# Attention layer on one core: later residues and roots, earlier row sums, and input rows added onto a second copy of the first product

## Chip, core and metric

The kernel runs on one core of one Trainium2 chip, as one launch. The metric is the device time of one execution in microseconds (us). In the profile PE is the matrix engine (TensorE), PEld its weight loads, DVE is VectorE, ACT ScalarE, POOL GpSimd and SP the queue that issues most transfers.

## The reference

One layer on 2048 tokens (a grid 64 wide) of width 1024, all in float32: a norm, one projection into q, k, v and gate, attention of each token over 8 rows by 16 columns of neighbours with a bias, a gate, an output projection, the residual sum and a last norm.

```python
g, w_in, rpb, w_out = layers[0]
h = rmsnorm(x, g)                          # y * rsqrt(mean(y*y) + 1e-6) * g
o, gate = neighbourhood_mixer(h, w_in, rpb)  # 16 heads of 64; softmax over 8 x 16 neighbours
x = x + (o * jax.nn.silu(gate)) @ w_out
return rmsnorm(x, norm_f)
```

## The kernel before

**Products.** Each float32 operand is split into a high part (rounded to the matrix engine's format) and a residue, and each product of two operands is made of three matmuls (high by high, high by residue, residue by high). Large products are made block by block as seven products of sums of blocks in place of eight (the products P stand in the order 1, 6, 2, 7, 5, 4, 3). A *form* `f` is a sum of blocks or a raw block, split for the matrix engine: ACT rounds it (`f<-raw`), DVE takes the residue (`f<-raw,f`). After a product DVE adds its bank to an earlier one (`u<-pp,acc`), or finishes an output.

**Order.** The kernel writes its whole order out: every engine runs its instructions in the order in which the program records them, with semaphores between engines. There is no scheduler. What a program line is recorded after is therefore what it stands behind on its engine.

**Stage one** (`stage_one`, to about 400 us) makes q, k, gate and values. `step(i)` records product i of a sequence, and `forms(i + lead)` makes the forms that many products ahead. `diagonal(c)` builds a diagonal matrix of row scales for `spread_rstd`: DVE writes `dg`, ACT rounds it to `dgh`, and DVE takes the residue `dgl`. **Stage two** (`stage_two`) goes on with the rest of the projections.

**Attention** runs in 32 cycles, one for each pair of heads and each eighth of the grid. A cycle records normalisation of the last scores, a filler of other matmuls on PE (`feed`, among them the output projection of the first row tiles, `po`), transposes `ph` of the probabilities (`turns`: PE transposes, three banks copied to `pta` by DVE and three by ACT), new scores `s`, and values `o`. The output projection of a row tile ends with `y<-po,xr` on DVE (bank plus input rows), a square with row sum on ACT, and then `finish(n)`: a *root* (eight short DVE rows of one column, lines 1457 to 1464, a reciprocal square root without ACT), a *scale* (two DVE rows of 512 columns, line 1472) and a *send*. `run_roots` and `run_scales` record what is due, once in a cycle: the scales first, of the roots that the last cycle made, then new roots. `rooted` holds the tiles that have a root and no scale yet.

**Output projection in pairs** (`rows_by_seven`, from about 905 us). Row tiles 6 to 15 are taken in PAIRS of two, each pair m as one block matrix of two rows by two columns, with the seven products `rows_product(m, P)`. The first three pairs are interleaved, and the last two follow. `on(i, f, ...)` records f behind step i of the sequence. `load_rows_of` loads a block of gated outputs, `sum_rows` makes S1 to S4, `form_rows` the forms, `add_rows` a finished output (`y<-py,...`, line 1430). `load_rest_of` loads input rows for the residual sum, `add_rest` adds them by an accumulating transfer on POOL onto a tile that holds a partial sum. `land_T2` and `land_T4` load sums of blocks of the weights. For these tiles the root takes three short DVE rows and a square root on ACT. `store(key, lag, f)` records f when a counter of finished work has moved on by `lag`.

Of the kernel before, what the change touches and what calls it, by code (L numbers as in the profile page):

```python
# [11 lines left out]
F32 = mybir.dt.float32  # L12
# [65 lines left out]
def build(ctx, tc, x, xr, xt, wg, bias, w_out, n0, nf, out):  # L78
# [141 lines left out]
    def diagonal(c, home=ev, late=False):  # L220
        dg = home([128, 512], F32, "dg")
        for i in range(4):
            to, f = dg[:, i * 128:(i + 1) * 128], rt[:, 4 * c + i:4 * c + i + 1]
            if late:
                nc.scalar.activation(to, ident, AF.Copy, scale=f)
            else:
                nc.vector.tensor_scalar(to, ident, f, None, op0=OP.mult)
        dgs[c] = h, l = home([128, 512], F32R, "dgh"), home([128, 512], F32R, "dgl")
        nc.scalar.activation(h, dg, AF.Copy)
        nc.vector.tensor_tensor(l, dg, h.bitcast(F32), OP.subtract)  # L230

    def spread_rstd(c):
        p = bank(512, "prb")
# [376 lines left out]
    def stage_one():  # L610
# [830 lines left out]
    def finish(n):  # L1441
# [129 lines left out]


    PAIRS = [(n, n + 1) for n in range(PLAIN, tiles - 2, 2)] + [(tiles - 1, tiles - 2)]
    A, F, B, U, R, T4 = {}, {}, {}, {}, {}, {}
    TF = {}
    plain_of = {"B11": (0, 0), "B21": (1, 0), "B22": (1, 1)}

# [42 lines left out]
    def load_rest_of(m, j, k):  # L1620
        n = PAIRS[m][j]
        RES[n, k] = (qp if (j, k) == (1, 0) else rbp)([128, 512], F32, "xr")
        nc.sync.dma_start(RES[n, k], x[n * 128:n * 128 + 128, 512 * k:512 * k + 512])

    def add_rest(n, j, to):
        nc.gpsimd.dma_start(to, x[n * 128:n * 128 + 128, 512 * j:512 * j + 512], accum_op=OP.add)

    def rows_product(m, P):
        n0, n1 = PAIRS[m]
        if P in (1, 6, 5):  # L1630
            B[m, P] = bank(512, "py")
            for Q in {1: (2,), 6: (7, 4), 5: (3,)}[P]:
                B[m, Q] = B[m, P]
        t = F.pop((m, P))
        f = uses[P][1]
        for k in range(4):
            c = slice(k * 128, k * 128 + 128)
            xh, xl = TF[f][k]
            for i, (a, b) in enumerate(((0, xh), (0, xl), (1, xh))):
                nc.tensor.matmul(B[m, P], t[:, a, c], b, start=P in (1, 6, 5) and k == 0 and i == 0, stop=k == 3 and i == 2,  # L1640
                                 skip_group_check=True)
                due(1)
        if P == 1:
            U[m, 1] = (xp if m == 2 else ep)([128, 512], F32, "p1")
            nc.scalar.activation(U[m, 1], B[m, 1], AF.Copy)
        elif P == 2:
            add_rows(n0, 0, B[m, 2])
        elif P in (6, 7):
            U[m, P] = xp([128, 512], F32, "u")
            nc.vector.tensor_tensor(U[m, P], B[m, P], U[m, 1], OP.add)  # L1650
            to = (n0, 1) if P == 6 else (n1, 1)
            if P == 6:
                RES[to] = U[m, 6]
                add_rest(n0, 1, U[m, 6])
            else:
                xr_ = RES.pop(to)
                nc.vector.tensor_tensor(U[m, 7], U[m, 7], xr_, OP.add)
                RES[to] = U[m, 7]
                add_rest(n1, 0, U[m, 1])
                RES[n1, 0] = U[m, 1]  # L1660
        elif P == 5:
            add_rows(n1, 1, B[m, 5])
        elif P == 4:
            add_rows(n1, 0, B[m, 4])
            finish(n1)
        else:
            add_rows(n0, 1, B[m, 3])
            finish(n0)

    def rows_by_seven():  # L1670
        for f, (r, c) in plain_of.items():
            TF[f] = [(woh[4 * r + k, c], wol[4 * r + k, c]) for k in range(4)]
        E, LEAD = 3, 5
# [7 lines left out]
        def on(i, f, *a):  # L1681
            todo.setdefault(i, []).append((f, a))
# [9 lines left out]
        for m in range(E, len(PAIRS)):  # L1692
            s = seq.index((m, 6)) - 1
            for d, f in ((-12, "A11"), (-10, "A21"), (-9, "A22"), (-7, "A12")) if m == E else \
                    ((-9, "A21"), (-8, "A22"), (-7, "A11"), (-6, "A12")):
                on(s + d, load_rows_of, m, f)
            for d, f in ((-5, "S1"), (-4, "S2"), (-3, "S3"), (-1, "S4")):
                on(s + d, sum_rows, m, f)
            on(s - 2, load_rest_of, m, 0, 0)
            on(s, load_rest_of, m, 1, 1)  # L1700
        for i, m in ((5, 0), (7, 1), (11, 2)):
            on(i, load_rest_of, m, 1, 1)
        for i, s in enumerate(seq):
            if i >= 2 * E:
                on(i - LEAD, form_rows, *s)
        for f in ("A21", "A22"):
            load_rows_of(1, f, vh)
        for m in range(E):
            load_rest_of(m, 0, 0)
        land_T4()  # L1710
        for m in range(E):
            form_rows(m, 2)
# [68 lines left out]
    for m in range(cycles + 1):  # L1781
# [3 lines left out]
        if m:  # L1785
            due_here = []
            quiet[0] = True
            if a < 12 and m > 8 and m % 2:
                normalise(2 * m - 1, True, lambda: due_here.append(split_rows() or consume(1, turn=True)))
            else:  # L1790
                normalise(2 * m - 1, True)
            run_scales()
            if a > 12:
                run_roots()
            elif not rows_due():
                run_roots(1)
# [12 lines left out]
        else:  # L1809
            feed(a * 0.6)  # L1810
# [61 lines left out]
```

## Time and profile before

| | |
|---|---|
| runs | 1009.82, 1009.84, 1011.5 us |
| median | 1009.84 us |
| profiled execution | 1009.61 us |
| its span | 1007.8 us, 1.8 us less than the execution |
| granted clock of PE | 0.999 |
| PE busy | 996.5 us, 6904 matmuls |
| DVE busy | 773.9 us |
| ACT busy | 519.4 us |
| POOL busy | 145.9 us |

A row of the timeline has start, duration, engine, line, operation, output and inputs, size and count; in brackets stands how long the engine was idle before it and what ended that. A row with a count over 1 groups neighbours that are alike.

### The profile page before, as it was taken

Reading aid. Unit: us, or ns where it says so; the run is one execution under the profiler, and the core shown is the slowest. Engines: PE = TensorE matmul, PEld = TensorE weight load, DVE = VectorE, ACT = ScalarE, POOL = GpSimd, SP = SyncE. Lnnn points to the kernel's source line nnn. Section 1 sums busy time; section 2 is a strip of 40 time slices with the busy share of each in tenths; the row PEclk is TensorE's granted clock in tenths of the full one; section 3 lists DMA queues with packets and bytes.
Section 4 is the critical chain, followed back from the end, with each engine's and each line's share of the span. In section 5 each row is a group of like instructions: output and inputs, shape, how many; then the busy total and the mean of one; then the engine's idle time right before and its main releaser. Section 6 shows DMA issues by size and latency. Waiting matters only on the chain. (4 is left out here: it accounts for less than half of the span.)

```text
span 1007.8 us, 19563 instructions
## 1 busy us (share of the span) xinstructions
PE 996.5 (99%) x6904; PEld 797.1 (79%) x6904; DVE 773.9 (77%) x1708; ACT 519.4 (52%) x1267; POOL 145.9 (14%) x228
## 2 busy tenths in 40 slices
PE   9999999999999999999999999999999999999997
PEld 6887888888888888888888777777777777778876
DVE  5899888987666866676765776778788888787876
ACT  7872244455534423343433465667767657563443
POOL 0000001321100000000000133233333323221100
PEclk9999999999999999999999999999999999999999
DMA  8945347777957755655566787879987679799453
GB/s 294 343 124 165 128 140 254 236 255 255 355 152 226 246 155 169 209 187 183 203 198 203 212 275 231 266 236 284 285 247 261 203 232 302 221 362 356 136 158 105
DMA packets 150122, 228.19 MB, mean 226 GB/s; under 512 B 13640, under 2 KB 65096, under 8 KB 150024
## 3 DMA queue, kind: packets, MB, share of 16 engines
q1 hardware_dynamic: 148152, 223.92, 69.1%
q0 software_dynamic: 1440, 2.62, 1.7%
q8 instruction: 54, 0.88, 0.3%
q10 hardware_dynamic: 432, 0.40, 0.1%
q14 instruction: 44, 0.36, 0.1%
HBM read 160.83 MB, written 66.06 MB: 225 GB/s over the span
## 5 line engine op out<-in xcount | busy, mean ns | idle before, releaser
L441 PE MATMUL pp<-h,f 128*128 128x512 f32 x576 | 185.3, 389 | 0.0
L1307 POOL TENSOR_SCALAR x<-x,st 128x360 f32<-128x360 f32 (+5 forms) x192 | 106.3, 570 | 530.0 <-DVE st L1300 529.7
L441 PE MATMUL pp<-t,f 128*128 128x512 f32 x702 | 171.9, 389 | 1.1 <-DVE u L454 1.1
L441 PEld LDWEIGHTS pp<-t,f 128*128 128x128 f32 x702 | 131.6, 188 | 29.2 <-ACT f L423 1.5
L1295 ACT ACTIVATE x<-x,st 128x360 f32<-128x360 f32 (+5 forms) x256 | 134.2, 526 | 26.4 <-DVE st L1289 26.4
L441 PEld LDWEIGHTS pp<-h,f 128*128 128x128 f32 x576 | 108.1, 188 | 22.4
L441 PE MATMUL pp<-l,f 128*128 128x512 f32 x288 | 112.1, 389 | 0.0
L1289 DVE CUSTOM_DVE_ANT_0 x<-s,em 128x360 f32<-128x360 f32 (+5 forms) x256 | 102.5, 454 | 2.1 <-PE s L1280 1.4
L424 DVE TENSOR_TENSOR f<-raw,f 128x512 fp32r<-128x512 f32 x105 | 75.6, 725 | 20.3 <-ACT f L423 20.2
L1354 PEld LDWEIGHTS o<-pta,vt 120*64 120x64 f32 (+2 forms) x1024 | 68.7, 137 | 22.7 <-DVE st L1289 15.2
L1354 PE MATMUL o<-pta,vt 120*64 120x192 f32 (+5 forms) x1024 | 83.4, 316 | 0.3 <-issue 0.3
L423 ACT ACTIVATE f<-raw 128x512 fp32r<-128x512 f32 x105 | 63.3, 622 | 38.3 <-DVE raw L430 22.3
L1324 DVE COPY pta<-ph 120x512 f32<-120x512 f32 (+5 forms) x96 | 56.0, 637 | 32.8 <-PE ph L1335 32.6
L1280 PE MATMUL s<-kt,q 64*64 64x360 f32 (+5 forms) x1024 | 78.8, 420 | 1.2 <-DVE y L1430 1.0
L1326 ACT ACTIVATE pta<-ph 120x512 f32<-120x512 f32 (+5 forms) x96 | 46.8, 558 | 62.5 <-PE ph L1335 62.4
L441 PEld LDWEIGHTS pp<-l,f 128*128 128x128 f32 x288 | 54.1, 188 | 11.3
L1280 PEld LDWEIGHTS s<-kt,q 64*64 64x64 f32 x1024 | 41.6, 131 | 23.1 <-ACT pta L1326 6.1
L605 PE MATMUL pv<-wh,t 128*128 128x512 f32 x176 | 56.2, 389 | 0.0
L441 PE MATMUL pp<-sixths,f 128*128 128x512 f32 x198 | 52.7, 389 | 0.0
L462 POOL TENSOR_TENSOR tmp<-tmp,rb 128x512 f32<-128x512 f32 x18 | 29.3, 1629 | 161.8 <-DVE tmp L459 132.7
L1640 PE MATMUL py<-woh,f 128*128 128x512 f32 x160 | 50.9, 390 | 0.9 <-DVE y L1430 0.9
L1335 PEld LDWEIGHTS ph<-ident,x 64*120 64x120 f32 (+2 forms) x1408 | 42.5, 128 | 11.3 <-issue 9.5
(222 smaller groups left out, 1864.2 us busy)
## 6 DMA issues: line engine op xcount, KB each, us to landing
raw<-in_wg_dram SPq DMA_DIRECT2D x124, 256.0 KB, 5.0
row<-in_xr_dram SPq DMA_DIRECT2D x34, 256.0 KB, 5.5
vd<-v SPq DMA_DIRECT2D x32, 256.0 KB, 3.4
sgd<-sg SPq DMA_DIRECT2D x32, 256.0 KB, 5.5
q<-qd SPq DMA_DIRECT2D x32, 256.0 KB, 5.6
sgt<-sgd SPq DMA_DIRECT2D x32, 256.0 KB, 6.6
ogd<-og SPq DMA_DIRECT2D x32, 256.0 KB, 3.3
kt<-kd SPq DMA_DIRECT2D x16, 480.0 KB, 6.6
```

Of the source, the lines that this page charges most:

```text
L423: nc.scalar.activation(t[:, 0], src, AF.Copy)
L424: nc.vector.tensor_tensor(t[:, 1], src, t[:, 0].bitcast(F32), OP.subtract)
L441: nc.tensor.matmul(B[n, P], t[:, int(m == 2), c], x[k][int(m == 1)], start=P in (1, 6, 5) and k == 0 and m == 0, stop=k == 3 and m == 2, s ...
L605: nc.tensor.matmul(p, a[:, o], b, start=P in (1, 6, 5) and k == 0 and m == 0, stop=k == 3 and m == 2, skip_group_check=True)
L1280: nc.tensor.matmul(pst[s][h * 64:h * 64 + 64], qt[a, g * 64:g * 64 + 64], kt[a, :r1 - r0, c0:c0 + 8 * WIDE[C]].rearrange("p r (s c) -> p s ...
L1289: nc.vector.tensor_tensor_reduce(X[i, C][s], pst[s], EM[p, ROW_TYPE[T]][C > 0][s], -1.0, 1e38, OP.add, OP.min, st[:, o:o + 1])
L1295: nc.scalar.activation(X[i, C][s], X[i, C][s], AF.Exp, bias=st[:, o:o + 1], scale=-1.0, accum_out=st[:, 4 + o:5 + o])
L1307: nc.gpsimd.tensor_scalar(X[i, C][s], X[i, C][s], st[:, o:o + 1], 1.0, op0=OP.mult, op1=OP.mult)
L1324: nc.vector.tensor_copy(o, i_)
L1326: nc.scalar.activation(o, i_, AF.Copy)
L1354: nc.tensor.matmul(o[s * 64:s * 64 + 64, g0 * 64:g1 * 64], vt[:k, strip, s * 64:s * 64 + 64], t[:k, n * 64:(n + g1 - g0) * 64], start=stri ...
L1640: nc.tensor.matmul(B[m, P], t[:, a, c], b, start=P in (1, 6, 5) and k == 0 and i == 0, stop=k == 3 and i == 2, skip_group_check=True)
```

## The change

It has four parts.

1. In stage one, the residue of the first diagonal is taken behind the two splits that follow it, and forms are made five products ahead instead of six in steps 21 to 32.
2. In an attention cycle that records a scale, no root is recorded; the root waits for the next cycle.
3. In the pairs, the row loads, the rests and the sums S1 and S2 are recorded sooner, in part ahead of the loads of T2, and scales and roots stand one count later.
4. The seventh product no longer gets its input rows by a second DVE sum. ACT makes a second copy of the first product (`xp1`), an accumulating transfer on POOL adds the input rows to it, and DVE adds the bank of the seventh product to that.

```diff
@@ diagonal
-        nc.vector.tensor_tensor(l, dg, h.bitcast(F32), OP.subtract)
+        def residue():
+            nc.vector.tensor_tensor(l, dg, h.bitcast(F32), OP.subtract)
+        if home is not ev:
+            return residue
+        residue()
@@ stage_one
-        diagonal(0, mp)
+        residue = diagonal(0, mp)
         step(4)
         split("T1", "x12", (2, 3), -1.0)
+        residue()
         step(5)
...
             step(i)
-            forms(i + (4 if i < 17 else 5 if i < 21 else 6))
+            forms(i + (4 if i < 17 else 5 if i < 33 else 6))
@@ finish
-            store(("y", n), 12, root)
-            store(("y", n), 12 if n == tiles - 2 else 24, scale)
+            store(("y", n), 12 if n >= tiles - 2 else 13, root)
+            store(("y", n), 12 if n == tiles - 2 else 25, scale)
@@ land_T2
+        for f in ("A21", "A22"):
+            load_rows_of(1, f, vh)
+        for m in range(LEADERS):
+            load_rest_of(m)
         land([("T2", k, i) for k in range(4) for i in range(2)], ...
@@ second copy
+    def second_p1(m, src):
+        V[m] = rbp([128, 512], F32, "xp1")
+        nc.scalar.activation(V[m], src, AF.Copy)
+        add_rest(PAIRS[m][1], 1, V[m])
@@ rows_product
             nc.scalar.activation(U[m, 1], B[m, 1], AF.Copy)
+            if m >= LEADERS:
+                second_p1(m, B[m, 1])
...
-            nc.vector.tensor_tensor(U[m, P], B[m, P], U[m, 1], OP.add)
+            nc.vector.tensor_tensor(U[m, P], B[m, P], U[m, 1] if P == 6 else V[m], OP.add)
...
-                xr_ = RES.pop(to)
-                nc.vector.tensor_tensor(U[m, 7], U[m, 7], xr_, OP.add)
@@ rows_by_seven
-                    ((-9, "A21"), (-8, "A22"), (-7, "A11"), (-6, "A12")):
+                    ((-10, "A11"), (-10, "A21"), (-10, "A22"), (-8, "A12")):
-            for d, f in ((-5, "S1"), (-4, "S2"), (-3, "S3"), (-1, "S4")):
+            for d, f in ((-6, "S1"), (-5, "S2"), (-3, "S3"), (-1, "S4")):
-            on(s - 2, load_rest_of, m, 0, 0)
-            on(s, load_rest_of, m, 1, 1)
-        for i, m in ((5, 0), (7, 1), (11, 2)):
-            on(i, load_rest_of, m, 1, 1)
+            on(s - 2, load_rest_of, m)
+        for i, m in ((4, 0), (5, 1), (7, 2)):
+            on(i, lambda m=m: second_p1(m, U[m, 1]))
@@ the attention cycles
+            most, behind = 99 if a > 12 else 0 if rows_due() else 1, bool(rooted)
             run_scales()
-            if a > 12:
-                run_roots()
-            elif not rows_due():
-                run_roots(1)
+            if not behind:
+                run_roots(most)
```

The lines of the changed kernel stand 6 to 19 lower than those of the kernel before.

**DVE in stage one, near 93 us of the profile.** `f` is a form's residue, `u` the sum that empties the bank of a product. Before:

```order
L430 TENSOR_TENSOR raw_969<-raw_969,s_973 128x512
L424 TENSOR_TENSOR f_1085<-raw_881,f_1085 128x512
L424 TENSOR_TENSOR f_1088<-raw_910,f_1088 128x512
L454 TENSOR_TENSOR u_1105<-pp_1091,acc0_174 128x512
L424 TENSOR_TENSOR f_1107<-s_944,f_1107 128x512
L454 TENSOR_TENSOR u_1124<-pp_1110,acc1_175 128x512
```

Now:

```order
L436 TENSOR_TENSOR raw_969<-raw_969,s_973 128x512
L430 TENSOR_TENSOR f_1085<-raw_881,f_1085 128x512
L460 TENSOR_TENSOR u_1102<-pp_1088,acc0_174 128x512
L430 TENSOR_TENSOR f_1104<-raw_910,f_1104 128x512
L460 TENSOR_TENSOR u_1121<-pp_1107,acc1_175 128x512
```

The form of raw_910 has moved behind the first `u`.

**DVE in the attention cycle whose transposes start at 848.86 us.** `gl` is the residue of two gated output blocks, `st3_8694` the statistics of a finished row tile, `y` an output with its input rows added, `pta` the copies of the transposes. Before:

```order
L1305 TENSOR_SCALAR x1_9919<-x1_9919,st_9906 128x288
L1401 TENSOR_TENSOR gl_9970<-ograw_9592,gh_9969 128x512 x2
L1430 TENSOR_TENSOR y_9975<-po_9765,xr_9233 128x512
L1324 COPY pta_9994<-ph1_9996 96x8x64
L1324 COPY pta_9994<-ph1_9998 96x8x64
```

Now:

```order
L1408 TENSOR_TENSOR gl_9958<-ograw_9584,gh_9957 128x512 x2
L1464 TENSOR_SCALAR st3_8694<-st3_8694 128x1
L1465 TENSOR_SCALAR st3_8694<-st3_8694 128x1
L1466 TENSOR_SCALAR st3_8694<-st3_8694 128x1
L1467 SCALAR_TENSOR_TENSOR st3_8694<-st3_8694 128x1
L1468 SCALAR_TENSOR_TENSOR st3_8694<-st3_8694 128x1
L1469 SCALAR_TENSOR_TENSOR st3_8694<-st3_8694 128x1
L1470 SCALAR_TENSOR_TENSOR st3_8694<-st3_8694 128x1
L1471 SCALAR_TENSOR_TENSOR st3_8694<-st3_8694 128x1
L1437 TENSOR_TENSOR y_9971<-po_9755,xr_9233 128x512
L1331 COPY pta_9990<-ph1_9992 96x8x64
```

The eight rows of this root have come in between `gl` and `y`. Before, they stood two cycles sooner, and in the cycle at 815.73 us the eight rows of the root of statistics 8367 stood between the scale of statistics 8161 and `y`; they are now in the cycle after it.

**DVE in the pairs, near 955 us.** `u_11428` takes the bank of the seventh product of pair 2, `s` is a row sum, the three rows of `st3` are a root, `y_11455` (now `y_11453`) reads the bank of the product (2,5). Before:

```order
L1612 TENSOR_TENSOR f_11406<-raw_11136,f_11406 128x512
L1451 TENSOR_SCALAR st3_11132<-st3_11132 128x1
L1453 RECIPROCAL st3_11132<-st3_11132 128x1
L1455 TENSOR_SCALAR st3_11132<-st3_11132 128x1
L1650 TENSOR_TENSOR u_11428<-py_11360,p1_11088 128x512
L1657 TENSOR_TENSOR u_11428<-u_11428,xr_11284 128x512
L1618 TENSOR_TENSOR s_11432<-s_11404,raw_11242 128x512
L1612 TENSOR_TENSOR f_11434<-s_11432,f_11434 128x512
L1472 SCALAR_TENSOR_TENSOR y_11133<-y_11133,st3_11132,acc0_174 128x512
L1472 SCALAR_TENSOR_TENSOR y_11402<-y_11402,st3_11132,acc1_175 128x512
L1430 TENSOR_TENSOR y_11455<-py_11437,u_11428 128x512
```

Now:

```order
L1437 TENSOR_TENSOR y_11404<-py_11290,u_11200 128x512
L1630 TENSOR_TENSOR s_11406<-s_11381,raw_11247 128x512
L1624 TENSOR_TENSOR f_11408<-raw_11136,f_11408 128x512
L1479 SCALAR_TENSOR_TENSOR y_11350<-y_11350,st3_11304,acc0_174 128x512
L1479 SCALAR_TENSOR_TENSOR y_11305<-y_11305,st3_11304,acc1_175 128x512
L1669 TENSOR_TENSOR u_11428<-py_11357,xp1_11204 128x512
L1624 TENSOR_TENSOR f_11430<-s_11406,f_11430 128x512
L1458 TENSOR_SCALAR st3_11132<-st3_11132 128x1
L1460 RECIPROCAL st3_11132<-st3_11132 128x1
L1462 TENSOR_SCALAR st3_11132<-st3_11132 128x1
L1437 TENSOR_TENSOR y_11453<-py_11433,u_11428 128x512
```

The second sum onto `u_11428` is gone, the row sum stands ahead of it, the scale of `st3_11132` has gone behind `y_11453`, and the scale of another tile (`st3_11304`) has come ahead of `u`.

More of the change, by code (lines that the diff above doesn't have):

```diff
@@ L1573, in build @@
     PAIRS = [(n, n + 1) for n in range(PLAIN, tiles - 2, 2)] + [(tiles - 1, tiles - 2)]
-    A, F, B, U, R, T4 = {}, {}, {}, {}, {}, {}
+    LEADERS = 3
+    A, F, B, U, V = {}, {}, {}, {}, {}
     TF = {}
@@ L1618, in sum_rows, with load_rest_of @@
         nc.vector.tensor_tensor(A[m, f], A[m, a], A[m, b], o)
[L1620 to L1623, printed above, removed]
+    def load_rest_of(m):
+        n = PAIRS[m][0]
+        RES[n, 0] = rbp([128, 512], F32, "xr")
+        nc.sync.dma_start(RES[n, 0], x[n * 128:n * 128 + 128, :512])
     def add_rest(n, j, to):
         nc.gpsimd.dma_start(to, x[n * 128:n * 128 + 128, 512 * j:512 * j + 512], accum_op=OP.add)
+    def second_p1(m, src):
+        V[m] = rbp([128, 512], F32, "xp1")
+        nc.scalar.activation(V[m], src, AF.Copy)
+        add_rest(PAIRS[m][1], 1, V[m])
     def rows_product(m, P):
@@ L1649, in rows_product @@
             U[m, P] = xp([128, 512], F32, "u")
-            nc.vector.tensor_tensor(U[m, P], B[m, P], U[m, 1], OP.add)
-            to = (n0, 1) if P == 6 else (n1, 1)
+            nc.vector.tensor_tensor(U[m, P], B[m, P], U[m, 1] if P == 6 else V[m], OP.add)
+            RES[(n0, 1) if P == 6 else (n1, 1)] = U[m, P]
             if P == 6:
-                RES[to] = U[m, 6]
                 add_rest(n0, 1, U[m, 6])
-            else:
-                xr_ = RES.pop(to)
-                nc.vector.tensor_tensor(U[m, 7], U[m, 7], xr_, OP.add)
-                RES[to] = U[m, 7]
                 add_rest(n1, 0, U[m, 1])
@@ L1672, in rows_by_seven @@
             TF[f] = [(woh[4 * r + k, c], wol[4 * r + k, c]) for k in range(4)]
-        E, LEAD = 3, 5
+        E, LEAD = LEADERS, 5
         seq = [(m, P) for P in (1, 2) for m in range(E)]
@@ L1705, in rows_by_seven @@
                 on(i - LEAD, form_rows, *s)
[L1706 to L1709, printed above, removed]
         land_T4()
```

## The prediction

> **What bounds the kernel now.** I read the page first, then the waits of TensorE (PE), then VectorE (DVE), ScalarE (ACT) and PE around each wait, row by row.
>
> ```profile
> span 1007.8 us, 19563 instructions
> PE 996.5 (99%) x6904; PEld 797.1 (79%) x6904; DVE 773.9 (77%) x1708; ACT 519.4 (52%) x1267; POOL 145.9 (14%) x228
> ```
>
> PE is busy for 996.5 of 1007.8 us. The change leaves PE's instructions, their count and their order as they are, so no matmul time can be gained: only the 11.3 us in which PE stands still can move. The last stretch shows where more than half of them lie (start and end, length, busy time of PE and the others):
>
> ```profile
> 1000.00:1008.00 8.00, 1.67 (x8) 1.05 (x6) 3.40 (x10) 3.29 (x10) 0.00 (x0) 0.92 0.35 133
> ```
>
> Some 6 us lie behind the last matmul, in a chain (last sum, square, root, scale, store) whose rows the change does not touch. The waits of PE (engine and line, who ended the wait, total us, times, longest) give the rest:
>
> ```profile
> PE pp L441 <- DVE u L454: 1.1, 1, 1.1
> PE s L1280 <- DVE y L1430: 1.0, 1, 1.0
> PE py L1640 <- DVE y L1430: 0.9, 1, 0.9
> ```
>
> Three waits, each happening once, each for a row of DVE, and the change has an edit near each. So the forecast is three small sums.
>
> **Stage one: forms later, residue later.** The first wait is at 95.31 us (start, duration, engine, line; in brackets the idle time before it):
>
> ```profile
> 93.27 1.28 DVE L424 TENSOR_TENSOR f<-raw,f 128x512 fp32r<-128x512 f32 x2
> 94.48 0.68 DVE L454 TENSOR_TENSOR u<-pp,acc 128x512 f32<-128x512 f32 x1
> 95.31 0.94 PE L441 MATMUL pp<-t,f 128*128 128x512 f32 x3 [1.09 <-DVE u L454]
> ```
>
> PE needs the bank that u (94.48 to 95.16) empties, and u stands behind two form residues f in a DVE queue without a gap. With a lead of 5 instead of 6 one f goes behind u: the two start at 93.27 and u at 94.48, so one is worth 0.60 us. That gain is partly used up 45 us earlier:
>
> ```profile
> 47.26 0.69 DVE L230 TENSOR_TENSOR dgl<-dg,dgh 128x512 fp32r<-128x512 f32 x1 [1.10 <-ACT dgh L229]
> 47.87 1.29 DVE L541 SCALAR_TENSOR_TENSOR t<-land,t 128x512 fp32r<-128x512 f32 x2
> 47.09 1.18 ACT L540 ACTIVATE t<-land 128x512 fp32r<-128x512 f32 x2
> ```
>
> Before, DVE idles 1.10 us for ACT's dgh, does the residue dgl, then the two t. After, the two t stand first. They wait for ACT's t rows, the first of which ends half way through 47.09 to 48.27, near 47.7, so they start at 47.75 instead of 47.87 and dgl comes behind them: the row at 49.08 starts at about 49.6. DVE is 0.5 us later, and being in deficit up to the wait it still is at 93 us. Net: −0.60 + 0.51, about **−0.1 us**. Bounds: −0.6 (a short DVE idle on the way absorbs the delay) and +0.1 (it does not and the residue costs its full 0.69). I take the sum, since I see only short idle stretches in between, both behind chains that shift too. The SP queue's loads of raw are asked for some 1 us later with buffers released later; I cost that at nothing, since they land over a step ahead.
>
> **Attention: the root leaves one cycle and enters another.** The second wait is in the cycle at 815.73:
>
> ```profile
> 814.30 1.71 DVE L1472 SCALAR_TENSOR_TENSOR y<-y,st,acc 128x512 f32<-128x512 f32 x2
> 815.92 0.20 DVE L1457 TENSOR_SCALAR st<-st 128x1 f32<-128x1 f32 x1
> 817.52 0.69 DVE L1430 TENSOR_TENSOR y<-po,xr 128x512 f32<-128x512 f32 x1
> 818.24 0.63 ACT L1433 ACTIVATE xr<-y 128x512 f32<-128x512 f32 x1 [5.14 <-DVE y L1430]
> 818.87 1.44 ACT L1326 ACTIVATE pta<-ph 120x512 f32<-120x512 f32 x3
> 815.73 1.51 PE L1335 MATMUL ph<-ident,x 64*120 64x64 f32 x44
> 818.26 3.40 PE L1280 MATMUL s<-kt,q 64*64 64x192 f32 x32 [1.02 <-DVE y L1430]
> 821.59 2.23 PE L1354 MATMUL o<-pta,vt 120*64 120x128 f32 x26
> ```
>
> DVE does the scale (two rows), the root (eight short rows, 815.92 to 817.52: 1.60 us) and only then y. ACT's square waits for y, ACT's copies stand behind the square, and the scores wait for the bank of y. A cycle that runs well, and that gets the root now:
>
> ```profile
> 846.75 1.50 DVE L1401 TENSOR_TENSOR gl<-ograw,gh 128x512 fp32r<-128x512 f32 x2
> 848.17 0.68 DVE L1430 TENSOR_TENSOR y<-po,xr 128x512 f32<-128x512 f32 x1
> 849.80 1.75 DVE L1324 COPY pta<-ph 96x512 f32<-96x512 f32 x3 [0.95 <-PE ph L1335]
> 848.89 0.63 ACT L1433 ACTIVATE xr<-y 128x512 f32<-128x512 f32 x1 [2.17 <-DVE y L1430]
> 849.60 1.46 ACT L1326 ACTIVATE pta<-ph 96x512 f32<-96x512 f32 x3
> 848.86 1.43 PE L1335 MATMUL ph<-ident,x 64*96 64x64 f32 x44
> 850.22 2.37 PE L1280 MATMUL s<-kt,q 64*64 64x192 f32 x32
> 852.52 1.25 PE L1354 MATMUL o<-pta,vt 96*64 96x128 f32 x14
> ```
>
> From the first transpose to the first value matmul it takes 3.66 us (848.86 to 852.52), and the cycle at 815.73 takes 5.86: it loses 2.2, of which I put 0.1 to its broader tiles (1.51 against 1.43), so 2.1.
>
> After, the order of the cycle at 815.73 is scale, y: y runs 815.92 to 816.60, the square at 816.64, ACT's copies near 817.27. They would start at 816.47 unhindered (0.74 behind the first transpose, as 849.60 to 848.86), so they are 0.8 late. What of this reaches the scores is between 0 (DVE's copies cover) and 0.8; I take 0.5. Gain 1.6.
>
> But the root for the tile of statistics 8694 now falls in the cycle at 848.86, between gl and y. There y moves by the root's 1.60, to run from 849.77 to 850.45; the square follows, and ACT's copies come 1.5 late at 851.1. In the disturbed cycle the first value matmul came 3.39 after y's end (821.59 − 818.20); 850.45 + 3.39 = 853.84 against 852.52: a new wait of 1.3. Bounds: 0.23 (only the scores' bank, free at 850.45 for 850.22) and 1.6 (all of it). I take 1.3, the nearest row being a cycle in just that condition. Every other cycle exchanges a root of 1.60 for a scale of about the same, or loses one of the two. The sends of y go out one or two cycles later on SP; nobody waits for them.
> Sum: −1.6 + 1.3 = **−0.3 us**, bounds −1.9 and +0.3.
>
> **Output projection: one sum less, scales later.** The third wait:
>
> ```profile
> 955.78 0.69 DVE L1657 TENSOR_TENSOR u<-u,xr 128x512 f32<-128x512 f32 x1
> 957.85 0.69 DVE L1612 TENSOR_TENSOR f<-s,f 128x512 fp32r<-128x512 f32 x1 [0.78 <-ACT f L1611]
> 958.46 1.41 DVE L1472 SCALAR_TENSOR_TENSOR y<-y,st,acc 128x512 f32<-128x512 f32 x2
> 959.78 0.68 DVE L1430 TENSOR_TENSOR y<-py,u 128x512 f32<-128x512 f32 x1
> 960.62 0.47 PE L1640 MATMUL py<-woh,f 128*128 128x512 f32 x1 [0.90 <-DVE y L1430]
> ```
>
> PE would have started at 959.56, one matmul's 0.23 behind the one at 959.33; it starts at 960.62, so it loses 1.06. Ahead of y go the second add onto u (0.61 to the next row), an idle 0.78 for a form whose sum is made a step sooner after, and the two scales (1.32 to y's start), which go behind y; a root of about 0.9 with its trip to ACT comes in front. 959.78 − 0.61 − 0.78 − 1.32 + 0.9 = 957.0, and with the scale of the row before now ahead of u, my walk through the new order gives 957.9 to 958.6: 0.9 ahead of 959.56. The wait goes: **−1.06 us**. Bounds: −1.06 and 0 (another row is late next). I take the whole, since DVE does one row less per pair there.
>
> For this the input rows of the seventh product are added by an accumulating DMA of GpSimd onto a second copy. Added are five ACT copies of 0.58 each (first row below; ACT is busy only 52% of the span) and five issues on POOL, whose price is in the accumulates that exist (duration in ns, minimum, median and maximum, then issue to landing):
>
> ```profile
> 961.19 0.58 ACT L1645 ACTIVATE p<-py 128x512 f32<-128x512 f32 x1
> L1626 POOL DMA_DIRECT2D u<-in_x_dram x5: 853/859/1018, 926.2 to 989.9; - x5
> DMA to landing us min/median/max: 3.7/4.5/5.8
> 926.92 0.39 PE L1640 MATMUL py<-t,f 128*128 128x512 f32 x1
> ```
>
> The product (0,7) runs from 926.92 for 2.72 us (12 matmuls, 0.227 apart). Its copy can be made near 918, so the accumulate lands by about 924 and is needed at 929.7: covered by 5 to 6 us.
>
> The loads of A21, A22 and three rests now stand on SP ahead of the eight T2 loads:
>
> ```profile
> 910.34 0.32 SPq L1581 DMA_DIRECT2D wol<-wodT  x1
> 910.93 0.92 SPq L1606 DMA_DIRECT2D raw<-ogd  x2
> DMA to landing us min/median/max: 5.1/5.1/5.1
> ```
>
> T2's last load (first row) is followed by the two raw 0.6 us later. At 0.6 to 0.65 us for each of the five loads, T2's last goes out 3.2 us later, at 913.5, and lands 5.1 later (third row, woh's loads in this stretch), near 918.7. PE first needs T2 with product (0,6), two products before 926.92, at 921.5. I cost it at nothing, with 2.8 us of cover.
>
> **The sum.** −0.1 − 0.3 − 1.06 = −1.4 us. The profiled execution took 1009.61 us (span 1007.8 and 1.8 around it), so it would take 1008.2; the median shown, 1009.84, lies 0.2 above it, so I forecast **1008.4 us**. A measurement of this kernel can tell about 0.2% (2.0 us) from no change; the forecast lies inside.
>
> **The rivals.**
> A, the covers hold: the copies at 848.86 are not late for the scores (0.23 instead of 1.3), and the residue costs nothing. Then −0.6 − 1.9 − 1.06 = −3.5 at best, 1006.3; with half of it 1007.2. For it: DVE idles 0.95 there before its copies. Against: ACT's copies stand behind a square that waits for y.
> B, nothing is gained in the output projection: the sums made sooner, or a scale put one product later, make the next y late, and PE loses the 1.06 two steps on. −0.1 − 0.3: 1009.4. For it: DVE is busy there, only 0.6 to 0.8 idle at a time. Against: a row less per pair.
> C, slower: GpSimd's accumulates. DVE is in order; if u of product seven waits for its copy, forms and sums queue behind it and PE follows. It decides where an accumulate takes over 10.5 us from issue to landing (4.5 median now, 5.8 at most), and each microsecond beyond costs one. Three of them now start between 916 and 926, where SP's loads are dense. At three times the median, 13.5, the price is 3 us or more: 1011.9 with the other gains kept at half. Against: no accumulate shown is over 5.8. The Trainium skill ("SBUF — State Buffer", section "SBUF: two separate sides") speaks for C: descriptors of a GpSimd DMA cannot be written while VectorE holds the shared port pair, and it gives some 3.1 us in place of 0.62 for one blocked in this way. The five accumulates above, issued in 0.85 to 1.02 us beside a DVE busy most of the time, do not show such a spread.
>
> **How the numbers follow.** Forecast 0.55, with a range of its own from 1007.4 to 1009.2; A 0.20, B 0.13, C 0.12. A reaches past 1007.8 nearly whole, and of the forecast's lower edge some 0.08 does: faster 0.27. C gives slower 0.12. The rest, 0.61, is the same. The range leaves out one in ten on each side: the better half of A lies below 1006.8, and C above 1010.3.
>
> **What would show it.** Right: no wait of PE for y near 960; PE's wait near 816 down to about half a microsecond, with a new one near 849 of 1.3 for y or the copies; u near 95 shifted by 0.1 only. Wrong: a PE wait on DVE u of product seven after 929, PE waiting for T2 near 921, DVE back in step at 66 us, or a cycle at 849 without a wait.

## The result and the profile after

| | before | after |
|---|---|---|
| median of 12 runs each | 1010.22 us | 1008.31 us |
| ratio to before, 95% interval | | 0.9981 (0.9972 to 0.999) |
| profiled execution | 1009.61 us | 1008.70 us |
| its span | 1007.8 us | 1006.6 us |
| end of the last matmul | 1001.67 us | 1000.16 us |

The change makes the kernel faster by 0.19% (1.9 us), at the edge of what I had called the same. The forecast was 1008.4, 1.4 us below the median then shown (1009.84); over all twelve executions that median is 1010.22.

The waits of PE in the changed kernel (engine and line, who ended the wait, total us, times, longest):

```profile
PE pp L447 <- ACT f L429: 1.3, 1, 1.3
PE s L1287 <- ACT pta L1333: 0.9, 2, 0.7
PE s L1287 <- DVE y L1437: 0.2, 1, 0.2
```

The wait for y in the output projection is gone, the one for y in attention has become three short ones for y and the copies, and the one near 95 us is 1.25 us long where it was 1.09. A wait of 1.2 us for `z` at the very start stands in both kernels; the forecast's list of three leaves it out, and the change does not touch it.

PE runs the same 6904 matmuls in the same order in both. So the start of each matmul after, less its start before, is a running account in which each step is a wait that came or went (between these places it drifts by up to 0.08):

| place (us) | account before it | account behind it | step | forecast |
|---|---|---|---|---|
| first 14 us | 0 | −0.09 | −0.09 | none |
| 95, `u` in stage one | −0.09 | +0.07 | +0.16 | −0.1 |
| 210, `u` behind a late load | +0.06 | −0.21 | −0.27 | none |
| 816, root gone | −0.17 | −1.77 | −1.60 | −1.6 |
| 849, root come | −1.76 | −0.43 | +1.33 | +1.3 |
| 960, output projection | −0.36 | −1.51 | −1.15 | −1.06 |

The tail behind the last matmul is 0.27 us longer; its rows on DVE and ACT keep their distances, and only the last store lands later.

**Stage one.** DVE in the changed kernel, then PE:

```profile
44.22 1.29 DVE L547 SCALAR_TENSOR_TENSOR t<-land,t 128x512 fp32r<-128x512 f32 x2
...
47.92 1.29 DVE L547 SCALAR_TENSOR_TENSOR t<-land,t 128x512 fp32r<-128x512 f32 x2 [1.62 <-ACT t L546]
49.13 0.68 DVE L232 TENSOR_TENSOR dgl<-dg,dgh 128x512 fp32r<-128x512 f32 x1
...
94.55 0.69 DVE L460 TENSOR_TENSOR u<-pp,acc 128x512 f32<-128x512 f32 x1
```

```profile
95.38 0.93 PE L447 MATMUL pp<-t,f 128*128 128x512 f32 x3 [1.25 <-ACT f L429]
```

The order did what was forecast: DVE idles 1.62 us for ACT's `t` instead of 1.10 for `dgh`, and dgl stands behind. The bracket on PE names an ACT form, but it was `u` that PE waited for: `u` ends at 95.24 and PE starts 0.14 later, as it started 0.15 behind `u` before. From the two `t` at 44 us to the start of `u` it is 50.33 us, against 50.39 before (44.09 and 94.48). But the two `t` start 0.13 later than before and PE comes 0.09 sooner; these 0.22, less the 0.06 of the order, are the +0.16 of the account.

**Attention.** The cycle that lost the root (DVE, ACT, PE):

```profile
815.76 0.68 DVE L1437 TENSOR_TENSOR y<-po,xr 128x512 f32<-128x512 f32 x1
```

```profile
817.10 1.44 ACT L1333 ACTIVATE pta<-ph 120x512 f32<-120x512 f32 x3
```

```profile
815.56 1.51 PE L1342 MATMUL ph<-ident,x 64*120 64x64 f32 x44
817.00 0.54 PE L1287 MATMUL s<-kt,q 64*64 64x192 f32 x2
817.73 2.17 PE L1287 MATMUL s<-kt,q 64*64 64x192 f32 x30 [0.19 <-ACT pta L1333]
819.82 2.39 PE L1361 MATMUL o<-pta,vt 120*64 120x128 f32 x28
```

It takes 4.26 us from the first transpose to the first value matmul (819.82 − 815.56) instead of 5.86. The cycle that got the root:

```profile
846.42 0.20 DVE L1464 TENSOR_SCALAR st<-st 128x1 f32<-128x1 f32 x1
...
848.01 0.68 DVE L1437 TENSOR_TENSOR y<-po,xr 128x512 f32<-128x512 f32 x1
```

```profile
847.10 1.43 PE L1342 MATMUL ph<-ident,x 64*96 64x64 f32 x44
848.75 0.54 PE L1287 MATMUL s<-kt,q 64*64 64x192 f32 x2 [0.22 <-DVE y L1437]
849.99 2.16 PE L1287 MATMUL s<-kt,q 64*64 64x192 f32 x30 [0.70 <-ACT pta L1333]
852.08 1.25 PE L1361 MATMUL o<-pta,vt 96*64 96x128 f32 x13
```

It takes 4.98 us instead of 3.66: the scores' bank is late by 0.2, and behind that the copies that stand behind the square of y.

**Output projection.** DVE near 957 us, then PE:

```profile
955.57 0.68 DVE L1669 TENSOR_TENSOR u<-py,xp 128x512 f32<-128x512 f32 x1
...
957.53 0.69 DVE L1437 TENSOR_TENSOR y<-py,u 128x512 f32<-128x512 f32 x1
```

```profile
958.97 0.61 PE L1657 MATMUL py<-woh,f 128*128 128x512 f32 x2
```

y ends at 958.22. The matmul that needs its bank is the second of the last row, 0.23 behind 958.97, at 959.20. It runs without a gap, 0.98 us behind y. The two stalls that the forecast feared for this part, at the T2 loads near 921 and at the copies near 929, are not there.

### The profile page after: what moved, and what is told of

It reads as the page before. It is cut to its first block, busy times and chain, and to the rows that moved or that the text cites. A ratio compares the mean times of both kernels' runs of the same rounds, so it can differ in the third digit from the quotient of the medians.

```text
span 1006.6 us, 19545 instructions
## 1 busy us (share of the span) xinstructions
PE 996.1 (99%) x6904; PEld 796.8 (79%) x6904; DVE 772.9 (77%) x1703; ACT 521.6 (52%) x1272; POOL 149.6 (15%) x233
## 4 chain that ended last, share of the span: by engine, by line
PE 97%; ACT 1%; DVE 1%; DMA 1%; SPq 0%; issue 0%
PE pp L447 40%; PE pv L611 13%; PE py L1657 9%; PE o L1361 8%; PE s L1287 7%; PE ph L1342 4%; PE pp L393 2%; PE pv L726 2%; PE pp L395 2%; PE pp L391 2%; PE po L1565 2%; PE po L1567 2%; PE po L1569 2%; DMA em<-in_bias_dram 1%; ACT x L1302 0%; PE zp L135 0%
```

## Experiments

All start from the changed kernel except the one that says otherwise. Ratios are to the kernel before on the same chip.

| run | ratio (95% interval) | median us | end of last matmul |
|---|---|---|---|
| changed kernel | 0.9981 (0.9972 to 0.999) | 1008.31 | 1000.16 |
| root back | 0.9994 (0.998 to 1.0007) | 1009.03 | 1001.61 |
| roots alone | 0.9969 (0.9957 to 0.9982) | 1006.96 | 998.60 |
| residue at once | 0.9977 (0.9964 to 0.9991) | 1007.98 | 999.03 |
| lead 4 | 0.9978 (0.9965 to 0.9991) | 1007.66 | 998.77 |
| second add | 1.0007 (0.9998 to 1.0016) | 1010.65 | 1000.99 |
| copy only, on the kernel before | 1.0004 (0.9991 to 1.0017) | 1009.83 | 1001.43 |
| lags back | 0.9988 (0.9978 to 0.9998) | 1008.31 | 999.73 |
| three edits | 0.9971 (0.9957 to 0.9984) | 1006.07 | 997.38 |
| changed kernel again | 0.9977 (0.9966 to 0.9988) | 1008.0 | 999.25 |
| three edits again | 0.9958 (0.9945 to 0.9971) | 1006.73 | 1000.06 |
| forms back, one execution | none | 1008.29 | 999.74 |
| sums back, one execution | none | 1014.31 | 1006.05 |

The effects are near the width of the intervals, so the verdicts rest on the places in the traces.

### The root in a cycle that scales

```diff
-            if not behind:
-                run_roots(most)
+            run_roots(99 if a > 12 else 0 if rows_due() else 1)
```

> The changed kernel, with a root again allowed in a cycle that scales. If the wait near 816 belongs to the root between scale and y, it comes back (the cycle from first transpose to first value matmul takes 5.8 to 5.9 us instead of 4.26) and the wait near 849 goes (3.66 instead of 4.99): net 0.2 us slower than the changed kernel, 1008.5 where that has 1008.3. If the gain near 816 came from something else (copies, buffers), the cycle near 816 stays at 4.3 us.

PE in that run:

```profile
815.26 1.51 PE L1342 MATMUL ph<-ident,x 64*120 64x64 f32 x44
817.78 4.65 PE L1287 MATMUL s<-kt,q 64*64 64x192 f32 x32 [1.01 <-DVE y L1437]
822.37 3.00 PE L1361 MATMUL o<-pta,vt 120*64 120x128 f32 x32
```

The wait is back and the one near 849 is gone, so the eight root rows are the cause at both places. But the cycle takes 7.11 us from first transpose to first value matmul, where 5.8 to 5.9 was expected. The windows of PE in that run (stretch, length, busy time of PE and the others, granted clock, DMA share, GB/s) show the difference:

```profile
816.00:818.00 2.00, 0.99 (x30) 0.82 (x24) 1.82 (x8) 0.24 (x1) 0.00 (x0) 1.00 0.96 316
818.00:820.00 2.00, 1.85 (x17) 0.70 (x19) 1.94 (x7) 2.00 (x6) 0.00 (x0) 0.95 0.57 212
820.00:822.00 2.00, 2.00 (x22) 1.16 (x16) 1.23 (x7) 1.56 (x7) 0.00 (x0) 0.50 0.81 171
822.00:824.00 2.00, 2.00 (x20) 1.45 (x18) 1.31 (x9) 2.00 (x9) 1.29 (x3) 0.70 0.83 315
```

Behind the wait PE's clock was granted at half for 3.4 us, and the account against the changed kernel goes from −0.34 to +2.91 at this cycle: 3.25 us, of which some 1.6 build up matmul by matmul at half clock. In the profiles of the kernel before and of the copy alone the same wait left the clock at 1.00, so in one of three profiles it cost twice what it did in the others.

For most timed executions the mean granted clock is known too. A stretch of 3.4 us at half clock takes 0.0017 off the mean of 1008 us, so 0.999 becomes 0.997. Means of 0.997 or less stand in 20 of 81 executions of the kernel before on three chips, in 2 of 10 of this run and in 2 of 10 of the copy alone, which all have the wait near 816. In the kernels without it (the changed one, and all runs from it but this one and the sums back, whose clock fell near 951) they stand in none of 91. On the chip of this run the kernel before took 1011.5 us on average where its mean was 0.997 (8 executions) and 1009.6 where it was 0.999 (11). So taking the wait away seems to take the loss of clock away with it; where in the kernel those executions lost it was not seen, since they were not profiled.

### Roots alone

```diff
-            if not behind:
+            if not behind and not any(due_here):
                 run_roots(most)
```

> The changed kernel, with a root allowed neither in a cycle that scales nor in one that has split gated output rows. If eight root rows between the residues gl and y make the wait near 849, it goes (3.66 us from first transpose to first value matmul instead of 4.99) and nothing comes in its place, since the root now goes into the next cycle, which held one before: 1.3 us faster than the changed kernel, about 1007.0. Rival: the wait moves on, because the last two roots and four scale rows now all fall in the start of the pairs (904 to 912 us): then PE waits there by up to 1.4 us and nothing is gained.

PE, then DVE, then PE again in that run:

```profile
847.11 2.37 PE L1287 MATMUL s<-kt,q 64*64 64x192 f32 x32
849.41 0.76 PE L1361 MATMUL o<-pta,vt 96*64 96x128 f32 x8
...
957.55 0.47 PE L1657 MATMUL py<-woh,f 128*128 128x512 f32 x1 [0.58 <-DVE y L1437]
```

```profile
934.38 0.69 DVE L1630 TENSOR_TENSOR s<-raw 128x512 f32<-128x512 f32 x1 [6.87 <-DMA raw<-ogd]
```

The wait near 849 goes and 1.3 us with it, as expected. But a new one comes near 957, worth 0.85 us by the account. It is neither of the two that the rival named: DVE idles 6.87 us for the row loads of the third pair, until 934.38, and its backlog reaches y at 957. Four stores now stand on SP ahead of these loads, where two stood, but the loads go out only 1.3 us later (the first at 921.47 instead of 920.22); they take 10.9 to 12.6 us to land, where they took 6.9 to 8.0. So the stores are at most a part of the cause.

### The residue and the forms

```diff
         residue = diagonal(0, mp)
+        residue()
         step(4)
         split("T1", "x12", (2, 3), -1.0)
-        residue()
```

> The changed kernel, with the first diagonal's residue taken at once, as before the change. If the later residue costs DVE 0.5 us that it never makes good before 95 us, u there ends 0.5 us sooner and the wait of PE near 95 falls from 1.25 us to 0.75; 0.5 us faster than the changed kernel. If the delay is absorbed on the way, the wait stays at 1.25.

PE's wait falls to 0.2 us, by more than the 0.5 expected. DVE in that run shows why:

```profile
43.47 1.29 DVE L547 SCALAR_TENSOR_TENSOR t<-land,t 128x512 fp32r<-128x512 f32 x2
...
46.65 0.69 DVE L232 TENSOR_TENSOR dgl<-dg,dgh 128x512 fp32r<-128x512 f32 x1 [1.10 <-ACT dgh L229]
47.26 1.29 DVE L547 SCALAR_TENSOR_TENSOR t<-land,t 128x512 fp32r<-128x512 f32 x2
```

DVE was 0.75 us sooner than in the changed kernel's profile at 43.47 already, ahead of anything that the edit touches: that start differs from one execution to the next. Taken from there, u starts 49.79 us later (93.26) instead of 50.33: the residue's place costs 0.54 us. The next two runs ask the same of the forms:

```diff
-            forms(i + (4 if i < 17 else 5 if i < 33 else 6))
+            forms(i + (4 if i < 33 else 5 if i < 45 else 6))     # lead 4, with the residue at once
+            forms(i + (4 if i < 17 else 5 if i < 21 else 6))     # forms back
```

> The changed kernel, with the residue at once and forms four products ahead up to step 32 (not five from step 17). One more form of 0.6 us then stands behind u: if each row of DVE ahead of u counts in full, the wait near 95 falls to about 0.15 us and this is 1.1 us faster than the changed kernel, about 1007.2. Rival: the chain of sums and outputs, not the forms, sets u: then the wait stays at 0.75, or forms made late give a new wait behind 95 us.

> The changed kernel with six products of lead for the forms from step 21 on, as before. In nine profiles the time from DVE's two t rows near 44 us to the start of u near 94 depends on the order alone: 50.41 before, 50.33 in the changed kernel, 49.80 with the residue at once, 49.19 with one more form behind u. If a form costs 0.60 and the residue 0.53, it is 50.93 here, and PE's wait near 95 is longer by 0.6 at the same start of DVE. If rows in between absorb it, it stays near 50.4.

In the run with lead 4 some forms are made after a later sum has overwritten their block, so part of its computation differs; the work is the same. Stage one's DVE clock in all profiles, from the start of the two `t` to the start of `u`:

| order of stage one | profiles | `t` starts at | to the start of `u` |
|---|---|---|---|
| before (residue at once, 6 from step 21) | 2 | 43.26, 44.09 | 50.43, 50.39 |
| changed (residue later, 5 to step 32) | 7 | 42.80 to 44.22 | 50.31 to 50.35 |
| forms back (residue later, 6 from step 21) | 1 | 43.25 | 50.93 |
| residue at once, 5 to step 32 | 3 | 43.29, 43.47, 42.98 | 49.82, 49.79, 49.98 |
| lead 4, residue at once | 1 | 44.02 | 49.19 |

(In the profile with 49.98 PE has no wait there, so DVE was not in arrears all the way.) The two edits are worth −0.60 and +0.54 and cancel. How long PE waits near 95 us is then a matter of when DVE and PE got going: with the changed order the wait is 1.25 where `t` starts at 44.22, 0.44 and 0.35 where it starts at 43.27 and 43.16, and 0.49 where it starts at 42.80, since PE came out of the first 14 us 0.7 sooner there than in the first of these. That spread of 1.4 us between executions is larger than anything the change does there.

### Output projection: the copy, the order or the lags

Second add:

```diff
-            if m >= LEADERS:
-                second_p1(m, B[m, 1])
...
-            nc.vector.tensor_tensor(U[m, P], B[m, P], U[m, 1] if P == 6 else V[m], OP.add)
+            nc.vector.tensor_tensor(U[m, P], B[m, P], U[m, 1], OP.add)
+            if P == 7:
+                nc.vector.tensor_tensor(U[m, 7], U[m, 7], V[m], OP.add)   # V[m]: input rows, loaded by SP
...
```

> The changed kernel with the seventh product's input rows loaded to a buffer of their own and added by a second DVE sum again; no second copy of the first product, no accumulating transfer for it. The sooner loads and sums and the later scales stay. If the order (scales behind y, sums sooner) took the wait near 960 away, one more DVE row of 0.61 us brings y from 958.2 to 958.8 us at its end, still before PE's 959.2: no wait there, the time that of the changed kernel within 0.3 us. If the second copy did it, PE waits there again by about a microsecond.

PE, then DVE in that run:

```profile
958.57 0.47 PE L1657 MATMUL py<-woh,f 128*128 128x512 f32 x1 [0.33 <-DVE y L1437]
...
995.26 0.47 PE L1657 MATMUL py<-t,f 128*128 128x512 f32 x1 [0.88 <-DVE u L1667]
```

```profile
955.04 0.69 DVE L1667 TENSOR_TENSOR u<-py,p 128x512 f32<-128x512 f32 x1 [0.51 <-DMA p<-in_x_dram]
...
994.43 0.69 DVE L1667 TENSOR_TENSOR u<-py,p 128x512 f32<-128x512 f32 x1 [1.26 <-PE py L1657]
```

A miss: by the account PE loses 0.57 us at the place, and 1.16 near the end that nobody expected. But neither is the price of the row. The kernel before sends the accumulating transfer of input rows onto the first copy `p` behind product seven, the changed kernel already behind product six, where product seven reads the second copy. This run puts the second sum back and leaves that transfer where it is. So product seven's `u`, which reads `p` again, waits until the transfer has landed, at 954.95 and at 994.33 (the bracket of the second row names PE), and takes those rows up as well, so part of its computation differs. Without the idle 0.51 us y would end at 957.91, 0.17 ahead of PE's 958.08: an estimate from these rows by which the row itself would cost next to nothing at this place. The run therefore does not tell the copy from the order. It does show the mechanism of rival C, product seven's `u` waiting for an accumulate.

Copy only, on the kernel before:

```diff
+            if m >= 3:
+                second_p1(m, B[m, 1])
...
-            nc.vector.tensor_tensor(U[m, P], B[m, P], U[m, 1], OP.add)
+            nc.vector.tensor_tensor(U[m, P], B[m, P], U[m, 1] if P == 6 else V[m], OP.add)
...
-                nc.vector.tensor_tensor(U[m, 7], U[m, 7], xr_, OP.add)
...
```

> The kernel before with only the second copy of the first product and its accumulating transfer, so without the second DVE sum; loads, sums and scales as before. If the order decides, y near 960 comes only 0.6 us sooner and PE's wait there falls from 1.06 to about 0.45 us: 0.6 us faster than the kernel before. If the copy is what counts, the wait goes: 1.06 us.

```profile
927.27 8.64 PE L1645 MATMUL py<-t,f 128*128 128x512 f32 x37 [1.08 <-DVE u L1657]
960.35 0.47 PE L1645 MATMUL py<-woh,f 128*128 128x512 f32 x1 [0.19 <-DVE y L1430]
```

```profile
917.96 0.69 DVE L1618 TENSOR_TENSOR s<-raw 128x512 f32<-128x512 f32 x1 [4.68 <-DMA raw<-ogd]
```

At 960 the wait falls from 0.90 to 0.19, about the one row of 0.61 us, as expected. At 927 a new one comes, 1.3 us by the account: the second pair's rows land at 917.9, 1.0 later than in the profile of before, and PE comes there 0.9 sooner, most of which it had from the first 14 us. So in the old order a gain made upstream is given back at a load. In the changed kernel, where these loads are issued ahead of T2, DVE does not wait for them.

Lags back:

```diff
-            store(("y", n), 12 if n >= tiles - 2 else 13, root)
-            store(("y", n), 12 if n == tiles - 2 else 25, scale)
+            store(("y", n), 12, root)
+            store(("y", n), 12 if n == tiles - 2 else 24, scale)
```

> The changed kernel with roots and scales of the pairs one count sooner again (12 and 24 instead of 13 and 25). If the scale's place behind y carries the gain, two scale rows of 1.32 us and perhaps a root come back ahead of y near 958 us, y ends near 959.5 and PE waits 0.3 to 0.5 us there. If the sums made sooner and the row less are enough, no wait.

No wait: y starts at 957.43, with the scale of its own place ahead of it and that of the place before no longer. It ends 0.64 us ahead of PE instead of 0.98. So the lags carry slack at this place and no wait. One run more took back the sums too:

```diff
-            for d, f in ((-6, "S1"), (-5, "S2"), (-3, "S3"), (-1, "S4")):
+            for d, f in ((-5, "S1"), (-4, "S2"), (-3, "S3"), (-1, "S4")):
```

> The changed kernel with the lags of roots and scales and the sums S1 and S2 of the last two pairs as before; the sooner row loads of the pairs and the second copy of the first product stay. If the sums made sooner are what took y near 960 ahead of PE beside the copy, DVE again idles 0.8 us for a form there and PE waits 0.4 to 0.5 us near 959; near 927, where the run with the copy alone waited 1.1 us for rows that landed late, there is no wait, since the loads stay ahead. If the copy and the loads are enough, no wait at either place.

That run settles nothing about the sums. In its profile DVE waited for the third pair's rows until 937.61, its forms were late, and PE waited 4.1 us for one near 951 and then ran at half clock for 3.4 us, 5.9 us lost in all (1014.31 us, a single run). How the 1.06 us divides between the copy, the sums and the loads thus stays open; the copy alone takes 0.7 of it in the old order, and the lags take none. DVE in the run with the sums back:

```profile
937.61 0.69 DVE L1630 TENSOR_TENSOR s<-raw 128x512 f32<-128x512 f32 x1 [7.48 <-DMA raw<-ogd]
```

### The three edits together

```diff
+        residue()                                   # at once, ahead of step(4)
-        residue()                                   # from behind the two splits
-            store(("y", n), 18, send)
+            store(("y", n), 70 if ended[0] else 18, send)
-            if not behind:
+            if not behind and not any(due_here):
```

> The changed kernel with three edits: the first residue at once; no root in a cycle that scales or that has split output rows; and the last two tiles' sends before the pairs 70 matmuls behind their scales instead of 18, so that they stand on SP behind the loads of the third pair's rows. If four stores ahead of these loads made the new wait near 957 of the run with roots alone, it goes now, and the wait near 849 stays away: 1.3 us less than the changed kernel by the root, 0.5 by the residue, about 1006.5. If the four scale rows on DVE were the cause, the wait near 957 stays at 0.6 to 0.8 us.

> The changed kernel itself, for comparison on the same chip: 0.998 of the kernel before, one wait near 95 us whose length goes with the start of DVE, waits of 0.4 near 817 and 1.3 near 849, none near 959.

> The changed kernel with the three edits again (first residue at once, roots alone in a cycle, later sends), on the same chip as the changed kernel: 1.3 us less by the wait near 849 and 0.5 by the residue, 1.8 us or 0.0018 of the time below it.

The first time PE had no wait over 0.3 us behind 800 us, and its last matmul ended 2.8 us sooner than in the changed kernel. The edits' own part of that is 1.3 near 849 and 0.5 by the residue; the rest is when the engines got going. On one chip the three edits had 0.9958 of the kernel before and the changed kernel 0.9977, with intervals that overlap a little, and the roots alone had 0.9969 on another. So this version is probably the fastest of those run, by some 1 to 2 us against the changed kernel. But the second profile of it, an execution of 1008.27 us, shows the same kernel with three waits in the output projection:

```profile
PE py L1657 <- DVE y L1437: 1.1, 2, 0.6
PE py L1657 <- ACT f L1623: 1.0, 1, 1.0
```

Again DVE had idled for the third pair's rows, 8.6 us, to 935.80, though the load that came at that time (issued at 920.32) now stood ahead of the stores. So moving the stores did not cure the wait. How these loads land (issue to landing, minimum, median, maximum us, each over the two loads whose landing the profile tells) in the profile of before, of the second add, of the changed kernel, of the three edits and of the three edits again:

```profile
DMA to landing us min/median/max: 5.0/5.5/6.0
```

```profile
DMA to landing us min/median/max: 5.2/5.4/5.5
```

```profile
DMA to landing us min/median/max: 6.9/7.4/8.0
```

```profile
DMA to landing us min/median/max: 5.2/7.2/9.1
```

```profile
DMA to landing us min/median/max: 12.2/13.8/15.4
```

Where no accumulates of the second copy run beside them, in the first two, they land in 5 to 6 us. Where these do, it takes 7 to 15, in all eleven profiles that have them (the 5.2 in the fourth line is a load issued ahead of them). The run with the second add has the loads as soon as the changed kernel, so it is not their order. In the kernel with the copy alone the accumulates start only at 923, and the loads had 5.2 to 6.1. The Trainium skill ("DMA: Bandwidth & Descriptors", section "Issuing engines are not separate DMA queues") says that transfers issued by SP and by GpSimd run on the same 16 engines and interleave; the traces agree, and show the price.

## Why the prediction was right

**Stage one** was right in both terms: the form was put at 0.60 and the profiles give 0.60; the residue at 0.51 and they give 0.54. The sum, −0.1, is the −0.08 by which u's distance changed. What the forecast did not have is the spread in the starts of DVE and PE, so PE's step there, +0.16, is not the sum.

**Attention**: +1.3 at 849 measured 1.33, by the walk that took the first value matmul to come 3.39 us behind y's end; it came 3.39 behind it (852.08 and 848.69). At 816 the 0.5 left of the 0.8 by which the copies are late was a choice between bounds, and the gain of 1.60 met it. What the forecast did not price is the clock: where the wait near 816 was followed by half clock it cost some 1.6 us more.

**Output projection**: the whole 1.06 came. y runs from 957.53 to 958.22, and as PE is 0.36 sooner there than before, that is 957.9 to 958.6 in the forecast's terms, the very figures of its walk. But the terms that it lists do not give them: 959.78 − 0.61 − 0.78 − 1.32 + 0.9 is 957.97 and not 957.0, and with the other scale's 1.32 ahead of u, y would have ended some 0.4 behind PE's 959.56. By the rows, u starts 0.87 later than before in these terms, and from u to y it takes 1.96 us instead of 4.72: the second add, the row sum, the idle time for its form and the scale are gone from there, and a root has come. The list leaves out the row sum (0.60), which went ahead of u as well, and the scale that came ahead delays u by 0.87 and not by its full 1.32. The run with the lags back shows that the two scales nearly cancel, 0.34 apart. So the walk was right and the sum written beside it was not.

**Covers**: the second copy's accumulates were put at 4.5 us to landing, and the copy that product (0,7) needs was to be there at 924. Over the five, landing took 7.5 in the median and 7.7 at most. So the one issued at 918.97 was there by 926.7, still 2.8 us ahead of `u` at 929.48. T2's cover held too: its last load went out at 912.88 and landed at 918.2, where 918.7 was forecast. In the changed kernel rival C had the right resource and the wrong victim: the accumulates were not late enough to be waited for, but the plain loads beside them were delayed, and in three of the profiles behind the result that made PE wait. The rule of the Trainium skill on the shared port ("SBUF — State Buffer", section "SBUF: two separate sides") was cited for C; no run here tells a blocked descriptor from a loaded engine.

**The total**: −1.4 forecast, −1.5 at the last matmul, −1.9 in the medians with an interval of −2.8 to −1.0. That the median of 1008.31 lies 0.1 from the forecast is in part luck: the kernel before turned out 0.4 slower than the three executions shown, and the change gained 0.5 more than the sum. At the last matmul, too, two steps that the forecast did not have, +0.16 at 95 and −0.27 at 210, nearly cancel. The −0.27 is a load that landed 1 us sooner; the run with the copy alone, which has the order of before there, shows the same step, so it is spread and not the change. If a quarter of the executions of the kernel before (20 of 81) lose some 1.7 us of clock near 816, that is 0.4 us of their mean, an estimate that would about close the gap between −1.5 and −1.9.

## What to carry to other kernels

Where PE is 99% busy, look for each wait by its place, and price an edit by what stands ahead of the late row on its engine: a row moved behind it is worth its duration, and a row moved into another full cycle can cost nearly as much there (1.60 gained and 1.33 paid for the root). An engine without slack carries a delay for 50 us unchanged, so a profile pair compares the edit and the start of the execution at once; measure from a row that the edit cannot touch. A sum taken off DVE by an accumulating transfer was paid for here by the loads beside it. And an experiment that puts one row back must put back the order of what that row reads, or it measures another wait.

## What the hardware showed that I had not expected

- Loads of 256 KB on SP, beside six accumulating transfers of GpSimd within 10 us in the changed kernel, took 7 to 15 us to land instead of 5 to 6. In that stretch the transfer engines stayed busy and moved less: before, then the changed kernel (stretch, length, busy time of the engines, clock, DMA share, GB/s):

```profile
920.00:930.00 10.00, 10.00 (x46) 8.29 (x45) 8.04 (x14) 5.30 (x12) 1.88 (x2) 1.00 1.04 354
```

```profile
920.00:930.00 10.00, 10.00 (x46) 8.29 (x45) 5.21 (x9) 4.86 (x11) 4.86 (x6) 1.00 1.09 322
```

- A wait of 1.0 us, in a cycle in which PE was busy for 0.99 of 2 us, was followed by 3.4 us at half clock in one profile (the root back) and by none in two others with the same wait. The copy alone is one of these, with PE busy for less (columns as above):

```profile
816.00:818.00 2.00, 0.92 (x18) 0.43 (x13) 1.90 (x7) 0.63 (x3) 0.00 (x0) 1.00 0.91 266
```

The Trainium skill ("TensorE: Matmul & The Clock Gate", section "HAM oscillation — how this bites in real kernels") puts the limit at idle gaps over about 3.4 us. The 4.1 us in the run with the sums back agrees, and its half clock lasted 3.4 us as well; the 1.0 us does not, and the runs leave open what decides.

- DVE's first 44 us differ by up to 1.4 us between executions of the same order, and from there to the start of `u` near 95 us it repeats to 0.05 us as long as PE waits for DVE there.
